# A fourth attention head's queries and keys in seven-product units, heads 40 steps apart, and small changes at the start and at the first convolution units

## The chip, the cores and the metric

The kernel runs on one core of a Trainium2 chip (eight cores, one used). The metric is the device time of one execution in microseconds, the median of several. Matmuls run on TensorE (PE, with weight loads shown as PEld), elementwise work on VectorE (DVE), ScalarE (ACT) and GpSimd (POOL); SyncE (SP) issues most DMAs.

## The reference

One streaming step of a one-layer hybrid encoder, in fp32, for 512 prompt frames and 64 sample frames (576 columns in all, D = 2048):

```python
hn = rmsnorm(x, g_norm1)
q, k, v, gb, gc, hc = jnp.split(hn @ w_in, ...)        # 6 x 1024 columns
q, k = rmsnorm(q, g_q), rmsnorm(k, g_k)                # per head, 8 heads x 128
o_attn = stick_breaking_blocks(q, k_all, v_all, P)     # weights: sigmoid(z) * prod(1 - sigmoid(z_j))
u = gc * hc
o_conv = gb * (conv_w[0]*u[t-2] + conv_w[1]*u[t-1] + conv_w[2]*u[t])
x = x + concat(rmsnorm(o_attn), rmsnorm(o_conv)) @ w_out
h2 = rmsnorm(x, g_norm2)
x = x + (silu(h2 @ w_gate) * (h2 @ w_up)) @ w_down     # D_FF = 5632
```

The sample frames also see 512 cached keys and values per head. Besides y the new keys, values and convolution states are outputs.

## The kernel before

Everything is kept transposed: channels on the 128 partitions, the 576 frames along the free axis in two halves of 288. A product of full precision is made from fp32r parts: an operand is split into a rounded high part (a ScalarE copy) and the remainder (a VectorE subtraction), and three matmuls (high x high, low x high, high x low) are summed.

**Plain projections.** `project` takes one 128-column weight through 2 halves x 16 k-tiles x 3 matmuls = 96 matmuls of 288 columns (`step`, L246). **Units.** Two columns at once can be made by a seven-product scheme (Strassen's, in Winograd's form): 7 products x 8 k-pairs x 3 = 168 matmuls (`unit_run`, L1047; `conv_run`, L1403; the feed-forward part, L1916). It needs sums of weight blocks (`unit_prepare`, `conv_prepare`) and sums of input blocks (`x_sums`, written to `xs_dram` by `store_sums` and read again by `load_sum` for the convolution part).

**Order.** PE's instructions are in the order of the program text. A `Pipeline` counts steps: `pipe.tick()` is called after each three matmuls, and generators that were spawned with a delay put out their next instructions at their step. So each engine's order follows from steps, and ACT, DVE, POOL and SP work through their own queues in order.

1. *Start* (L425 to L509). x arrives by column chunks (`XCH`), is turned by PE transposes (`turn_x`, L390), copied by ACT (L399, L401), scaled and split by DVE (L408, L409). The first projection's k-steps follow with a lag of three tiles, except that steps 0 and 1 run at tiles 1 and 3. Sums of squares of x (`square`, L419 on DVE for the last two chunks, L422 on ACT for the others) follow one by one, most of them after the loop.
2. `EARLY`: q and k of heads 0 and 1 as plain projections, stored to `qk_dram`.
3. `UNIT_COLS`: four units: v of heads 0 to 5 and q, k of head 2. Their weight blocks lie in five places that `call_blocks` refills.
4. `LATE`: twelve plain columns: q, k of heads 3 to 7 and v of heads 6, 7. Meanwhile `attend(h)` runs for all eight heads, head h spawned at step 1 + 49 h (`PERIOD`), each over 116 steps. Inside it `until(t)` waits to step t of that head. Its stations, by step before the change: load q and k (E, 0), cached keys (6), squares on ACT (8, 10), sums over 32 channels on DVE (12), their sum on PE (`ss`, L795, 22), the norm on DVE (23 to 29), scaling and splitting of q and k (30 to 35), key stores on SP (36), scores (48 to 55, L844 and L868), three logarithm steps on ACT for each key block, splits (55 to 64), sums over later keys (72, 75, 78: L919 to L937), each followed by `limit` (a mask on DVE, L893, an exponential on ACT, L895, and a cast), the last splits (76 to 81), the output product `po` (90, L951 and L954), the sample rows' sum `cz` (100) and product `os_` (112).
5. Two convolution groups as plain projections; after the first half of the third column `open_b` frees the heads' tiles and loads `xs_t1` and `xs_t2`.
6. Convolution units in the order of `corder`; after the first product `load_sum(3)` loads the last sums. `call_columns` loads weight columns (L1338) when a place is free.
7. Output projection, then gate and up units, then down units.

The change touches 1 (`square`, the loop), 3 (`UNIT_COLS`, `first_units`), 4 (`LATE`, `PERIOD`, `attend`, `late_evac`) and 6 (`load_sum` and its call).

Of the kernel before, what the change touches and what calls it, by code (L numbers as in the profile page):

```python
# [10 lines left out]
F32 = mybir.dt.float32  # L11
# [87 lines left out]
def tile_hybrid_stream_step(  # L99
# [314 lines left out]
    def square(c, i):  # L414
# [3 lines left out]
        if i < 4 and c >= len(XCH) - 2:  # L418
# [7 lines left out]
    with tc.manual_schedule(engines={mybir.EngineType.Activation, mybir.EngineType.DVE, mybir.EngineType.SP}):  # L426
# [3 lines left out]
        w0h, w0l = ready[0]  # L430

# [21 lines left out]
        for kt in range(KD + LAG):  # L453
# [22 lines left out]
            for c, (k0, k1) in enumerate(XCH):  # L476
# [274 lines left out]
    late_E = {}  # L751

    def attend(h):
# [9 lines left out]
        f, hi, lo, E = {}, {}, {}, {}  # L763
        for n, c in (("q", 0), ("k", 1)):
            if (c, h) in late_E:
                E[n] = late_E[c, h]
            else:
                E[n] = t1.tile([P, T], F32, tag="E" + n, name="E" + n)
                nc.sync.dma_start(out=E[n], in_=qk_dram[2 * h + c])
# [8 lines left out]
        yield until(8)  # L778
        for i, n in enumerate("qk"):
            if i:  # L780
                yield until(10)
            if (i, h) in EARLY:
                nc.vector.transpose(out=E[n], in_=E[n])
            f[n] = t1.tile([P, T], F32, tag=n + "f", name=n + "f")
            nc.scalar.activation(out=f[n], in_=E[n], func=AF.Square)
        yield until(12)
        for i, n in enumerate("qk"):
            nc.vector.reduce_sum(out=sums[:, NB * i : NB * (i + 1)], in_=chunks(f[n]), axis=mybir.AxisListType.X)
# [1481 lines left out]
```

## Time and profile before

| | |
|---|---|
| time, median of 3 runs | 2334.69 us (2334.25 to 2334.76) |
| the profiled execution | 2334.58 us, span 2332.9 us |
| PE busy | 2319.2 us (99%), 17445 matmuls |
| DVE busy | 1909.2 us (82%) |
| ACT busy | 1163.7 us (50%) |
| POOL busy | 278.5 us (12%) |
| HBM read, written | 303.23 MB, 95.86 MB |

A busy row is the union of an engine's instructions over the span. Matmuls overlap: each shows some 294 ns, though they start 132 ns apart. In the timeline a row has its start, its length, engine, line, operation, tiles written and read, sizes and count; in brackets stands the idle time of the engine ahead of it and what ended it. The groups have busy time and mean nanoseconds after the bar. The windows give, for each stretch, its length, then busy time (and instructions) of PE, PEld, DVE, ACT and POOL, the granted clock, the DMA engines' share and GB/s. By position the stages are: start 0 to 32 us, early projections to 72, units to 161, late projections with the heads to about 413, convolution to about 755, output projection to about 857, then feed-forward.

### The profile page before, as it was taken

To read this page: it belongs to the slowest core of one execution; us is meant where nothing else is said; L and a number is where in the kernel's file an instruction comes from. 1 tells how busy PE (TensorE), PEld (TensorE's weight loads), DVE (VectorE), ACT (ScalarE), POOL (GpSimd) and SP (SyncE) were. 2 spreads that over 40 slices of the span, in tenths; PEclk is the share of its full clock that TensorE was granted. 3 is DMA by queue.
4 is the path that set the end of the run, shared out by engine and by line. 5 is a ranking of instruction groups with operands and counts; after the bars stand their busy time and mean duration, and the time that the engine had idled before them with its cause. 6 is when DMAs were issued, how large, how long until landed. Compare 5 with 4: busy or idle time off the path is not lost.

```text
span 2332.9 us, 43682 instructions
## 1 busy us (share of the span) xinstructions
PE 2319.2 (99%) x17445; PEld 2309.7 (99%) x17445; DVE 1909.2 (82%) x2844; ACT 1163.7 (50%) x2007; POOL 278.5 (12%) x392
## 2 busy tenths in 40 slices
PE   9999999999999999999999999999999999999999
PEld 8999999999999999999999999999999999999999
DVE  8977776888887899888888888888888777887886
ACT  7537776444445565444444444444444444444444
POOL 2002332121111220000000000000000001431121
PEclk9999999999999999999999999999999999999999
DMA  8775554963478554444444444354344936885553
GB/s 276 208 226 144 142 142 127 309 199 106 129 245 247 166 174 144 155 129 149 142 138 153 125 151 156 110 158 150 123 154 135 363 114 214 220 239 192 198 135 101
DMA packets 584580, 401.93 MB, mean 172 GB/s; under 512 B 91775, under 2 KB 571769, under 8 KB 584377
## 3 DMA queue, kind: packets, MB, share of 16 engines
q1 hardware_dynamic: 573944, 378.27, 52.0%
q0 software_dynamic: 10064, 20.65, 3.9%
q8 instruction: 136, 2.23, 0.4%
q14 instruction: 68, 0.55, 0.1%
q10 hardware_dynamic: 368, 0.24, 0.0%
HBM read 303.23 MB, written 95.86 MB: 171 GB/s over the span
## 4 chain that ended last, share of the span: by engine, by line
PE 92%; DVE 4%; DMA 2%; ACT 2%; issue 1%; SPq 0%; POOL 0%; ACTq 0%; DVEq 0%; POOLq 0%
PE psy L1916 36%; PE psw L1916 18%; PE psx L1916 9%; PE pj L246 8%; PE psy L1403 6%; PE pjo L246 4%; PE psw L1403 3%; PE psy L1047 2%; PE psx L1403 1%; PE psw L1047 1%; PE psx L1047 1%; DMA Eq<-qk_dram 1%; DVE wlo L208 1%; DMA raw_a<-in_w_in_dram 0%; PE z L844 0%
## 5 line engine op out<-in xcount | busy, mean ns | idle before, releaser
L1916 PE MATMUL psy<-h_s,whl 128*128 128x288 f32 x2787 | 411.0, 294 | 0.0
L1916 PEld LDWEIGHTS psy<-h_s,whl 128*128 128x128 f32 x2787 | 383.4, 188 | 0.0
L256 DVE TENSOR_TENSOR whl<-raw_a,whl 128x1024 fp32r<-128x1024 f32 (+4 forms) x296 | 316.5, 1070 | 57.9 <-ACT whl L255 56.7
L1916 PE MATMUL psw<-t,whl 128*128 128x288 f32 x2400 | 347.6, 295 | 0.0
L1916 PEld LDWEIGHTS psw<-t,whl 128*128 128x128 f32 x2400 | 327.9, 188 | 0.2 <-DVE whl L256 0.2
L255 ACT CAST whl<-raw_a 128x1024 fp32r<-128x1024 f32 (+4 forms) x296 | 268.0, 906 | 101.6 <-issue 35.1
L246 PE MATMUL pj<-x,whi 128*128 128x288 f32 x1376 | 296.9, 299 | 0.4 <-DVE x L409 0.2
L256 DVE TENSOR_TENSOR whl<-raw_b,whl 128x1024 fp32r<-128x1024 f32 (+5 forms) x190 | 199.6, 1051 | 66.1 <-ACT whl L255 65.3
L255 ACT CAST whl<-raw_b 128x1024 fp32r<-128x1024 f32 (+5 forms) x190 | 165.4, 872 | 165.5 <-issue 73.1
L1926 ACT COPY part<-psy 128x288 f32<-128x288 f32 x242 | 96.6, 399 | 283.0 <-PE psy L1916 279.7
L246 PEld LDWEIGHTS pj<-x,whi 128*128 128x128 f32 x1376 | 227.7, 189 | 2.0 <-DVE x L409 1.1
L246 PE MATMUL pj<-x,wlo 128*128 128x288 f32 x688 | 203.7, 296 | 0.7 <-DVE wlo L182 0.6
L1916 PE MATMUL psy<-t2t,whl 128*128 128x288 f32 x1212 | 183.0, 294 | 0.0
L1916 PE MATMUL psy<-b22m,whl 128*128 128x288 f32 x1212 | 182.5, 294 | 0.0
L1916 PE MATMUL psx<-h_s,whl 128*128 128x288 f32 x1185 | 173.3, 294 | 0.0
L1916 PEld LDWEIGHTS psy<-t2t,whl 128*128 128x128 f32 x1212 | 168.2, 188 | 0.2 <-DVE whl L256 0.2
L1916 PEld LDWEIGHTS psy<-b22m,whl 128*128 128x128 f32 x1212 | 168.0, 188 | 0.0
L1916 PEld LDWEIGHTS psx<-h_s,whl 128*128 128x128 f32 x1185 | 162.6, 188 | 0.0
L246 PEld LDWEIGHTS pj<-x,wlo 128*128 128x128 f32 x688 | 129.7, 189 | 1.9 <-DVE wlo L182 0.9
L255 ACT CAST whl<-s 128x1024 fp32r<-128x1024 f32 (+5 forms) x81 | 72.3, 893 | 102.3 <-PE psw L1916 102.3
L1695 POOL DMA_DIRECT2D hid_dram<-form x3 | 2.3, 759 | 971.1 <-DVE form L256 971.1
L1916 PE MATMUL psy<-t,whl 128*128 128x288 f32 x576 | 106.8, 295 | 0.0
(534 smaller groups left out, 4482.5 us busy)
## 6 DMA issues: line engine op xcount, KB each, us to landing
hid_dram<-form SPq DMA_DIRECT2D x147, 288.0 KB, 2.5
raw_a<-in_w_in_dram SPq DMA_DIRECT2D x33, 1024.0 KB, 5.6
raw_a<-in_w_gate_dram SPq DMA_DIRECT2D x22, 1024.0 KB, 5.5
raw_a<-in_w_up_dram SPq DMA_DIRECT2D x22, 1024.0 KB, 5.6
raw_b<-in_w_gate_dram SPq DMA_DIRECT2D x22, 1024.0 KB, 6.4
raw_b<-in_w_up_dram SPq DMA_DIRECT2D x22, 1024.0 KB, 7.7
h_s<-hid_dram SPq DMA_DIRECT2D x10, 2016.0 KB, 11.3
raw_a<-in_w_out_dram SPq DMA_DIRECT2D x16, 1024.0 KB, 5.5
```

The costliest lines, as they stand in the source:

```text
L208: nc.vector.tensor_tensor(out=lo[:, a : a + 1024], in0=raw[:, a : a + 1024], in1=hi[:, a : a + 1024].bitcast(F32), op=ALU.subtract)
L246: mm(ps, w_[:, k, csl], x_, start=(k == 0 and n == 0), stop=(k == nk - 1 and n == 2))
L255: nc.scalar.copy(out=hi, in_=src)
L256: (lo_eng or nc.vector).tensor_tensor(out=lo, in0=src, in1=hi.bitcast(F32), op=ALU.subtract)
L1047: mm(ps, whl[:, w_, j, :], x_, start=(start and j == 0 and q == 0), stop=(j == NP - 1 and q == 2), skip_group_check=True)
L1403: mm(ps, whl[:, w_, j, :], x_, start=(start and j == 0 and q == 0), stop=(j == m - 1 and q == 2), skip_group_check=True)
L1695: q.dma_start(out=hid_dram[fp][2 * n - 2 : 2 * n].rearrange("f p t -> p f t"), in_=t.bitcast(F32))
L1916: mm(ps, whl[:, w_, j, :], x_, start=(start and j == 0 and q == 0), stop=(j == len(xs_) - 1 and q == 2), skip_group_check=True)
L1926: nc.scalar.copy(out=t, in_=st["y"])
```

## The change

- `UNIT_COLS` has a fifth unit, q and k of head 3; `LATE` loses these two columns and has another order. The places of the first weight blocks are called in another order.
- `PERIOD` is 40 and the stations in `attend` move; a head takes 109 steps. q and k are loaded apart, the squares go to a scratch area, and the key of head 7 is stored and loaded as the others are. The scaled fp32 copies of q and k, which had 576 columns, are kept for the last 192 columns alone: ACT writes the rounded copy straight from the unscaled one with the scale, and DVE makes the low part with the scale in a `scalar_tensor_tensor`.
- At the start eight products of a matrix of ones with itself are put in (5, 1 and 2), steps 0 and 1 of the first projection move to tiles 3 and 4, and the squares of the last chunk but one go from DVE to ACT.
- `load_sum(3)` is issued in two halves, after the first and the third product.

```diff
-UNIT_COLS = [[(2, 0), (2, 1)], [(2, 2), (2, 3)], [(2, 4), (2, 5)], [(0, 2), (1, 2)]]
+UNIT_COLS = [[(2, 0), (2, 1)], [(2, 2), (2, 3)], [(2, 4), (2, 5)], [(0, 2), (1, 2)], [(0, 3), (1, 3)]]
-LATE = [(0, 3), (1, 3), (0, 4), (1, 4), (0, 5), (1, 5), (2, 6), (0, 6), (1, 6), (0, 7), (1, 7), (2, 7)]
-PERIOD = 49
+LATE = [(0, 4), (1, 4), (0, 5), (1, 5), (0, 6), (1, 6), (0, 7), (1, 7), (2, 6), (2, 7)]
+PERIOD = 40
...
-        if i < 4 and c >= len(XCH) - 2:
+        if i < 4 and c == len(XCH) - 1:
...
+        warm = ps_pj.tile([P, HALF], F32, tag="pj", name="warm")
+        def keep_warm(n):
+            for _ in range(n):
+                mm(warm[:, :P], onef, onef, start=True, stop=True)
...
+                    keep_warm(1)
                     heads_of["s"] = turn_samples(0)
...
+                keep_warm(5)
                 turn_x(0, 0, 0, 0, None, first)
...
+            if kt == 2:
+                keep_warm(2)
...
-            k = {1: 0, 3: 1, 4: None}.get(kt, kt - LAG)
-            if k is not None and k >= 0 and (k or kt == 1):
+            if kt >= LAG:
                 for i, ps in enumerate(q0ps):
-                    step(ps, w0h, w0l, slice(0, P), x_two, k, KD, i)
+                    step(ps, w0h, w0l, slice(0, P), x_two, kt - LAG, KD, i)
...
+        def square_sums(i, n, t):
+            if (i, h) in EARLY:
+                nc.vector.transpose(out=E[n], in_=E[n])
+            sq = scratch[:, :T]
+            nc.scalar.activation(out=sq, in_=E[n], func=AF.Square)
+            yield until(t)
+            nc.vector.reduce_sum(out=sums[:, NB * i : NB * (i + 1)], in_=chunks(sq), axis=mybir.AxisListType.X)
+        fetch(0, "q")
         yield until(6)
+        fetch(1, "k")
+        yield until(9)
+        yield from square_sums(0, "q", 11)
+        yield until(14)
+        yield from square_sums(1, "k", 16)
+        yield until(18)
         cK = t1.tile([P, TP], F32, tag="cK", name="cK")
...
-        yield until(22)
+        yield until(24)
         ss = misc("ss")[:, : 2 * NB]
...
-        yield until(25)
+        yield until(27)
...
-            yield until(27 + 2 * i)
+            yield until(29 + 2 * i)
...
-        yield until(30)
-        nc.scalar.activation(out=qf, in_=qf, func=AF.Copy, scale=gqs)
-        cast(qh, qf[:, :TP])
-        yield until(32)
-        nc.scalar.activation(out=kf, in_=kf, func=AF.Copy, scale=col("gk"))
-        cast(kh, kf[:, : 3 * P])
-        yield until(33)
-        low(ql, qf[:, :TP], qh)
-        yield until(35)
-        low(kl, kf[:, : 3 * P], kh)
-        yield until(36)
-        nc.vector.transpose(out=cK, in_=cK)
+        for t, n, w in ((32, "q", gqs), (34, "k", col("gk"))):
+            yield until(t)
+            nc.scalar.activation(out=hi[n], in_=f[n][:, : cut[n]], func=AF.Copy, scale=w)
+            nc.scalar.activation(out=end[n], in_=f[n][:, 3 * P :], func=AF.Copy, scale=w)
+            yield until(t + 2)
+            stt(out=lo[n], in0=f[n][:, : cut[n]], scalar=w, in1=hi[n].bitcast(F32), op0=ALU.mult, op1=ALU.subtract)
+        yield until(37)
         put_tokens(E["k"], kp[:, h, :], 0, TP)
         put_tokens(E["k"], ks[:, h, :], TP, T)
+        yield until(39)
+        nc.vector.transpose(out=cK, in_=cK)
...
-        yield until(84)
+        yield until(82)
         sh = t1.tile([P, T], F32R, tag="sph", name="sph")
...
-        yield until(90)
+        yield until(87)
         po = misc("po")
...
-        yield until(100)
+        yield until(95)
         cz = misc("cz")
...
-        yield until(112)
+        yield until(105)
         os_ = misc("os")
...
-        call_blocks((2, 0, 1, 3, 4))
+        call_blocks((0, 2, 3, 4, 1))
...
-    def load_sum(q):
-        t = bt[q] = bt["pool"].tile([P, NP, 2, HALF], F32R, tag=f"t{q}", name=f"xs_t{q}")
-        nc.sync.dma_start(out=t.bitcast(F32), in_=xs_dram[q].rearrange("j f p t -> p j f t"))
+    def load_sum(q, j0=None):
+        if not j0:
+            bt[q] = bt["pool"].tile([P, NP, 2, HALF], F32R, tag=f"t{q}", name=f"xs_t{q}")
+        j0, j1 = (0, NP) if j0 is None else (j0, j0 + 4)
+        nc.sync.dma_start(out=bt[q][:, j0:j1].bitcast(F32), in_=xs_dram[q, j0:j1].rearrange("j f p t -> p j f t"))
...
-        if k_ == 0:
-            load_sum(3)
+        if k_ in (0, 2):
+            load_sum(3, k_ * 2)
```

The steps from 48 to 81 (scores, splits, sums over later keys, masks) stay where they were.

More of the change, by code (lines that the diff above doesn't have):

```diff
@@ L762, in attend, with fetch @@
         sums, ms, y, t_ = (scratch[:, 1856 + 36 * q : 1892 + 36 * q] for q in range(4))
[L763 to L769, printed above, removed]
+        f, hi, lo, E, end = {}, {}, {}, {}, {}
+        cut = {"q": TP, "k": 3 * P}
         def chunks(t, w=32):
             return t.rearrange("p (b c) -> p b c", c=w)
-        yield until(6)
+        def fetch(i, n):
+            E[n] = t1.tile([P, T], F32, tag="E" + n, name="E" + n)
+            nc.sync.dma_start(out=E[n], in_=qk_dram[2 * h + i])
+        def square_sums(i, n, t):
[6 more added lines that the diff above has]
+        fetch(0, "q")
+        yield until(6)
+        fetch(1, "k")
[4 more added lines that the diff above has]
+        yield until(18)
         cK = t1.tile([P, TP], F32, tag="cK", name="cK")
@@ L777, in attend @@
                               in_=ck[:, h, 32 * q : 32 * (q + 1)].rearrange("(b t) c -> t b c", t=32))
[L778 to L783, printed above, removed]
-            f[n] = t1.tile([P, T], F32, tag=n + "f", name=n + "f")
[L785 to L788, printed above, removed]
-        for n, e in (("q", TP), ("k", 3 * P)):
-            hi[n] = t1.tile([P, e], F32R, tag=n + "h", name=n + "h")
-            lo[n] = t1.tile([P, e], F32R, tag=n + "l", name=n + "l")
-        qf, qh, ql, kf, kh, kl = (x[n] for n in "qk" for x in (f, hi, lo))
-        yield until(22)
+        for n in "qk":
+            f[n] = t1.tile([P, T], F32, tag=n + "f", name=n + "f")
+            hi[n] = t1.tile([P, cut[n]], F32R, tag=n + "h", name=n + "h")
+            lo[n] = t1.tile([P, cut[n]], F32R, tag=n + "l", name=n + "l")
+            end[n] = t1.tile([P, T - 3 * P], F32, tag=n + "e", name=n + "e")
+        qf, qh, ql, qe, kf, kh, kl, ke = (x[n] for n in "qk" for x in (f, hi, lo, end))
+        yield until(24)
         ss = misc("ss")[:, : 2 * NB]
@@ L840, in scores @@
             if i == 3:
[L841 removed]
+                mm(zb[i], ke[:, :P], qe[:, :P], stop=False, **kw)
                 return
@@ L946, in attend @@
         cast(sh, sp)
-        yield until(86)
+        yield until(84)
         low(sl, sp, sh)
-        yield until(90)
+        yield until(87)
         po = misc("po")
@@ L1121, in evac @@
         def evac(ps, a, b):
-            if (c, h) == (1, NH - 1):
-                if not a:
-                    late_E[c, h] = t1.tile([P, T], F32, tag="Ek", name="Ek")
-                nc.vector.transpose(out=late_E[c, h][:, a:b], in_=ps)
-                return
             count[0] += 1
```

12 lines of the change are left out of this document (5 added, 7 removed).

## The prediction

> **What bounds the kernel now.** I read the page first (engines, chain), then PE's waits, then the timeline round each wait.
>
> ```profile
> span 2332.9 us, 43682 instructions
> PE 2319.2 (99%) x17445; PEld 2309.7 (99%) x17445; DVE 1909.2 (82%) x2844; ACT 1163.7 (50%) x2007; POOL 278.5 (12%) x392
> ```
>
> PE is busy 99% of the span and all else is behind it; a saved matmul shortens the run and a saved VectorE (DVE) or ScalarE (ACT) instruction does not, unless PE waits for it. What a matmul costs is read from the chain of waits, in order of time (start, length, what):
>
> ```profile
> 84.90 3.17 PE psy L1047 x24
> 423.38 39.55 PE pj L246 x299
> 476.12 11.65 DMA raw_a<-in_w_in_dram
> ```
>
> 24 matmuls take 3.17 us in a seven-product unit, 299 take 39.55 us in a plain projection: 132 ns each in both (the 294 ns that the groups show is latency). A step of the planner, three matmuls, is 0.40 us. PE's waits over the whole run (total, times, longest):
>
> ```profile
> PE psy L1403 <- DVE whl L1375: 2.1, 2, 1.3
> PE po L954 <- ACT ph L738: 0.7, 2, 0.4
> PE ss L795 <- DVE raw_a L788: 0.5, 1, 0.5
> ```
>
> So besides the matmul count only three places can give time: the start, the first convolution units and the heads. The profiled execution took 2334.58 us (span 2332.9 and 1.7 around it), the median of the three runs is 2334.69; I carry the sum over to the median.
>
> **Part 1, the fourth head's q and k in a unit.** Two plain columns are 2 x 2 x 16 x 3 = 192 matmuls, a unit is 7 x 8 x 3 = 168. 24 x 0.132 = **-3.17 us**. The unit adds some eight 128x1024 VectorE sums and splits against four splits; the units' stretch and one head period show whether they are hidden:
>
> ```profile
> 72.00:161.00 89.00, 89.00 (x675) 89.00 (x674) 72.77 (x92) 33.88 (x45) 2.18 (x4) 1.00 0.75 210
> 208.76:236.92 28.16, 28.16 (x210) 27.80 (x208) 21.60 (x40) 22.28 (x43) 7.12 (x17) 1.00 0.49 127
> ```
>
> Four units run there with PE never idle, DVE at 82%, ACT at 38%. A fifth is like them: nothing to add.
>
> **Part 2, the start.** PE's first x transposes, the first projection matmuls among them, and DVE's matching work:
>
> ```profile
> 3.81 1.09 PE L390 MATMUL psx<-ident,xin 128*128 128x128 f32 x4 [3.81 <-POOL acA L298]
> 8.60 0.61 PE L246 MATMUL pj<-x,wlo 128*128 128x288 f32 x1 [0.57 <-DVE wlo L182]
> 9.97 1.91 PE L390 MATMUL psx<-ident,xin 128*128 128x128 f32 x8
> 12.99 1.09 PE L390 MATMUL psx<-ident,xin 128*128 128x128 f32 x8
> 11.80 0.52 DVE L408 TENSOR_SCALAR x<-st,g1c 128x576 fp32r<-128x576 f32 x1 [1.86 <-ACT st L401]
> L373 SPq DMA_DIRECT2D xin<-in_x_prompt_dram x1: 507/507/507, 2.4 to 2.4; - x1
> DMA to landing us min/median/max: 5.7/5.7/5.7
> ```
>
> The transposes of tiles 2 and 3 run at 9.97 although their x, issued at 2.4, landed 5.7 us later, at 8.1: they stand behind step 0, which waits for a weight's low part. DVE then idles 1.86 us, and is dense from there to the end of the x tiles. After the change step 0 stands behind tile 3, so the transposes start at about 8.2 and DVE goes on at once. The eight transposes also take 1.91 us here and 1.09 us later: PE runs slow this early. The eight filler products lie in gaps: five before 3.81, the others before x of samples and tile 2 has landed.
>
> ```profile
> L868 PE MATMUL zs<-qf,cK 128*128 128x128 f32 x64 | 8.5, 275 | 0.0
> ```
>
> An fp32 128x128 product shows as two instructions of 133 ns, so eight are 2.1 us, perhaps 4 us at the slow rate; cover is 3.8 + 0.5 us. Without it they would cost the excess. The Trainium skill (TensorE: Matmul & The Clock Gate, Part 1: The HAM clock gate) has the array at half clock until about 3.4 us of sustained work. By that rule the fillers open the gate before tile 2; the slow transposes agree, though the granted clock of every window reads 1.00.
>
> Against it: four 128x512 squares go from DVE to ACT.
>
> ```profile
> 33.29 0.69 DVE L419 SCALAR_TENSOR_TENSOR xin<-xin 128x512 f32<-128x512 f32 x1
> 36.20 0.61 ACT L422 ACTIVATE xsn<-xsn 64x512 f32<-64x512 f32 x1
> 41.52 1.22 DVE L208 TENSOR_TENSOR wlo<-raw_a,whi 128x1024 fp32r<-128x1024 f32 x1
> 45.21 0.29 PE L246 MATMUL pj<-x,whi 128*128 128x288 f32 x1
> ```
>
> A square's time goes by its free size (512), so that is 4 x 0.61 = 2.4 us more in ACT's queue, ahead of the third weight's casts; DVE, 2.4 us lighter, waits for ACT's sums at the same place. The third weight's first low half is done at 42.74 for matmuls from 45.21: a slack of 2.5 us, which the 2.4 us use up. So of up to 1.9 us I take **-1.5 us** (ends -2.1 and 0).
>
> **Part 3, the last convolution sums in two halves.**
>
> ```profile
> 473.00:482.00 9.00, 9.00 (x70) 9.00 (x69) 8.06 (x8) 4.45 (x6) 0.00 (x0) 1.00 1.08 390
> 487.80 1.23 DVE L1361 TENSOR_TENSOR raw_a<-raw_a,raw_c 128x1024 f32<-128x1024 f32 x1 [1.62 <-DMA raw_a<-in_w_in_dram]
> 492.74 3.33 PE L1403 MATMUL psy<-xs_t,whl 128*128 128x288 f32 x23 [0.86 <-DVE whl L1375]
> 499.37 2.35 DVE L1375 TENSOR_TENSOR whl<-raw_a,whl 128x1024 fp32r<-128x1024 f32 x2
> 500.65 5.56 PE L1403 MATMUL psy<-x,whl 128*128 128x288 f32 x40 [1.27 <-DVE whl L1375]
> ```
>
> The weight column of the chain's DMA row (issued 476.12, landed 487.77) stands behind the sums' 8 x 2 x 128 x 288 x 4 = 2.36 MB. With half of that behind it, it lands 1.18 MB / 390 GB/s = 3.0 us sooner, DVE's 1.62 us wait goes, and with it PE's first stall. The second stall stays nearly whole: from 491 DVE works without a gap to the split at 499.37, which moves up by about as much as PE does. The second half has until product 4, at 494 or later. Gain 0.86 to 1.6: **-1.4 us** (ends -2.5, both stalls, and 0).
>
> **Part 4, heads 40 steps apart.** Nine steps fewer per head take 3.6 us off the 28.2 us of the period shown above; it holds 21.6 us of DVE, 22.3 of ACT. After: 24.6 us, DVE some 20.7 (9/32 of a column's two splits and two transposes less, 0.9), ACT at most 21.7. Nothing saturates; the order inside a head decides. Head 0's output product waited like this:
>
> ```profile
> 198.27 0.34 PE L937 MATMUL z<-s0l,neg1r 128*128 128x384 f32 x1
> 203.22 0.27 DVE L893 SCALAR_TENSOR_TENSOR z<-z,acA 128x128 f32<-128x128 f32 x1
> 203.24 0.38 PE L951 MATMUL po<-pr,vtok 128*128 128x128 f32 x2
> 204.16 0.34 PE L954 MATMUL po<-pl,vh 128*128 128x384 f32 x1
> 204.80 0.76 DVE L741 TENSOR_TENSOR pl<-pr,ph 128x512 fp32r<-128x512 f32 x1 [0.48 <-ACT ph L738]
> 204.82 0.50 PE L954 MATMUL po<-ph,vh 128*128 128x512 f32 x1 [0.32 <-ACT ph L738]
> ```
>
> The scores are complete at 198.61, but DVE masks them only at 203.22, 4.6 us later, behind the next head's norm (steps 23 to 29 of that head). From mask to last split are 2.3 us. With 40 steps that norm falls at steps 64 to 71, before the masks; in their place stand two low parts (0.7 and 0.6 us), so the mask runs 0 to 1.6 us late. The output product comes three steps (1.2 us) earlier. From the end of the scores to its last operand there are then 9 x 0.40 us and the products ahead of that operand (203.24 to 204.16 and three more, 1.5 us); less the 2.3 that leaves 2.8 us for the mask's lateness, so these stalls go. Head 0's first sum has its VectorE chain two steps longer and two steps later; its wait shrinks:
>
> ```profile
> 165.62 0.78 DVE L783 STREAM_TRANSPOSE Eq<-Eq 128x576 f32<-128x576 f32 x1 [4.03 <-DMA Eq<-qk_dram]
> 169.88 0.74 DVE L788 TENSOR_REDUCE raw_a<-kf 128x18 f32<-128x576 f32 x1
> ```
>
> It now blocks the weight's low half (1.2 us), which in the new order goes ahead of it. Together some 2 us go (the waits view's 1.2, and 0.2 to 0.3 more for each, since it counts idle from the modelled end of the last matmul: 204.16 to 204.82 lost 0.48, not 0.32).
>
> What comes: a head's squares and sums (steps 9 to 16) now fall among the previous head's scores, whose logarithms fill ACT. PE wants the key's sum eight steps (3.2 us) after it is put out, where it was ten.
>
> ```profile
> L205 ACT CAST whi<-raw_a 128x1024 fp32r<-128x1024 f32 x23 | 22.9, 1043 | 0.0
> ```
>
> A weight's two casts (2.1 us) stand at step 7 of each column of 32, a head starts at 1 + 40h: in heads 2 and 6 they fall on its step 54 (81 + 54 = 128 + 7), just before the next head's key square, and I take 1 us lost in each, at the sum or at the sample rows' product. Also all loads of a next head stand behind eight key stores on SP:
>
> ```profile
> 205.04 4.83 SPq L726 DMA_DIRECT2D out_dram<-Ek  x8
> 210.03 0.35 SPq L769 DMA_DIRECT2D Eq<-qk_dram  x1
> ```
>
> Issued at step 37 they last to step 47, so q's load starts some 3 us late and lands about when its square is due at step 9. Scaling into the rounded copies and 192 columns takes ACT from 2048 to 1280 columns a head; PE does not feel it. I set stalls gone against stalls new: **0 us** (ends -2, nothing new, and +6, a new 1 us in every head).
>
> **Sum:** -3.17 - 1.5 - 1.4 + 0 = -6.1: 2334.69 - 6.1 = **2328.6 us**.
>
> **Rivals.** *The heads take some back (0.2):* every head waits 0.6 us at its sum or at the product for the sample rows, 8 x 0.6 - 2 = +2.8: 2331.4. For it: the work packed into the score window; against it: PE never idles in the period shown, with much the same work. *Only the matmuls go (0.17):* ACT's squares eat the start, and the weight's load is held by its own wait on DVE, not by the queue: 2334.69 - 3.2 = 2331.5. *The masks stay late (0.07), slower:* if DVE's backlog before the last mask keeps head 0's 4.6 us in all heads, past the 2.8 us that are left, each head loses 1.8 us, 14.4 - 2 = +12.4 against -6.1: 2341.0. For it speaks POOL:
>
> ```profile
> 175.89 1.73 DVE L741 TENSOR_TENSOR ql<-qf,qh 128x512 fp32r<-128x512 f32 x1
> 175.83 1.24 POOL L810 TENSOR_TENSOR Ek<-Ek,rpad_t 128x576 f32<-128x576 f32 x1 [3.88 <-ACT qh L738]
> ```
>
> Beside POOL's key scaling this split of 512 columns took 1.73 us; one of the same size took 0.76 alone (204.80). After the change the scaling falls right before the masks. The Trainium skill (Advanced Engine Details and Errata, VectorE Performance Modes, Mode Summary) says that the second Vector SBUF port is shared with GpSimd and the two block each other; by it this delay returns in every head, about 1 us, which is under the 2.8. The pair of rows agrees.
>
> **Chances.** Forecast 0.56, its own range 2326 to 2330.5. 0.2% is 4.7 us, about what a measurement of this kernel can tell from no change; faster means under 2330.0. The forecast case lies there nearly always (0.52), the second and third in a third of their cases (0.06): faster 0.58; slower 0.07; same 0.35. Range: the low end adds the better ends of parts 2 to 4 in part (-9), the high end takes in both middle rivals and part of +6: 2325.7 to 2334.0.
>
> **What would show it.** Right: 24 fewer unit and projection matmuls beside eight filler products; DVE with no gap near 10 us; no wait of DVE on the weight's DMA near 480 and one PE stall, not two, in the first convolution units; no wait on the ph cast in the heads. Wrong: PE waits at sums in most heads, masks over 2.8 us behind their scores, or ACT's casts late for the third projection.

## The result and the profile after

The changed kernel takes 2357.18 us (median of 5 runs, 2354.72 to 2358.92); the kernel before, beside it, 2334.69. The ratio is 1.0094, 95% interval 1.0083 to 1.0105: slower by 22.5 us where 6 us less were forecast. The profiled execution took 2357.18 us. Its page, span and engines:

```profile
span 2355.1 us, 43712 instructions
PE 2329.8 (99%) x17437; PEld 2314.5 (98%) x17437; DVE 1916.4 (81%) x2846; ACT 1163.5 (49%) x2021; POOL 273.8 (12%) x394
```

The matmuls are 8 fewer: 24 fewer for the unit, 16 more instructions for the fillers, as announced. Everything else has to be looked for by stage. Windows cut at the first unit matmul, the last one, the first matmul of the convolution units and their last (columns: window, length, busy time and count of PE, PEld, DVE, ACT and POOL, granted clock, DMA share, GB/s). First the kernel before:

```profile
0.00:72.05 72.05, 66.26 (x479) 63.56 (x479) 63.44 (x140) 55.13 (x149) 13.27 (x30) 1.00 0.83 275
72.05:160.77 88.72, 88.72 (x674) 88.72 (x672) 72.72 (x92) 33.83 (x45) 2.18 (x4) 1.00 0.74 210
160.77:462.88 302.11, 300.73 (x2215) 295.80 (x2214) 226.71 (x415) 200.53 (x389) 81.62 (x154) 1.00 0.61 172
462.88:754.96 292.08, 289.95 (x2190) 289.37 (x2189) 233.81 (x326) 135.15 (x217) 49.98 (x60) 1.00 0.62 187
```

and then the changed one:

```profile
0.00:73.57 73.57, 70.00 (x495) 67.26 (x495) 59.83 (x130) 57.17 (x155) 13.34 (x30) 1.00 0.83 269
73.57:184.50 110.93, 110.93 (x842) 110.93 (x840) 89.50 (x112) 42.61 (x56) 4.34 (x8) 1.00 0.68 193
184.50:484.30 299.80, 284.69 (x2023) 274.63 (x2022) 217.89 (x404) 189.50 (x384) 76.78 (x151) 0.98 0.59 165
484.30:777.00 292.70, 290.62 (x2190) 289.48 (x2189) 234.73 (x329) 135.42 (x218) 46.96 (x62) 1.00 0.62 188
```

- The start is 1.5 us longer (73.57 against 72.05).
- The units are 22.2 us longer, which is one unit, 88.72 / 4, with PE never idle: hidden, as forecast.
- The head stage has lost 192 matmuls, 192 x 0.132 = 25.4 us, so it should take 302.1 - 25.4 = 276.7 us. It takes 299.8: **23.1 us are lost there**, the whole loss of the run. PE is idle for 15.1 us of the stage, and the mean granted clock is 0.98.
- The convolution units are 0.6 us longer (292.70 against 292.08); the gain forecast for them does not show in this one execution.

Where PE stands, in the waits of the changed kernel (total, times, longest):

```profile
PE po L964 <- DVE pl L750: 10.4, 14, 2.1
PE ss L808 <- DVE raw_a L786: 3.2, 2, 2.9
PE os L984 <- issue: 1.4, 2, 0.7
...
PE ps_r1s L532 <- DVE rpad_t L523: 1.0, 1, 1.0
```

The output product waits 14 times for the last splits; before it waited twice, 0.7 us. What holds the splits is seen round the masks of one head, head 3. A head has three masks; the last one's scores are complete at 307.01, and this is what "late" is counted from below. DVE in the changed kernel:

```profile
306.23 0.60 DVE L903 SCALAR_TENSOR_TENSOR z<-z,acA 128x128 f32<-128x128 f32 x2
308.50 0.75 DVE L830 SCALAR_TENSOR_TENSOR ql<-qf,gqs,qh 128x512 fp32r<-128x512 f32 x1 [1.68 <-ACT qh L827]
309.17 0.29 DVE L903 SCALAR_TENSOR_TENSOR z<-z,acA 128x128 f32<-128x128 f32 x1
309.37 0.61 DVE L830 SCALAR_TENSOR_TENSOR kl<-kf,vec,kh 128x384 fp32r<-128x384 f32 x1
...
310.24 0.29 DVE L903 SCALAR_TENSOR_TENSOR z<-z,acA 128x128 f32<-128x128 f32 x1
...
312.79 1.23 DVE L208 TENSOR_TENSOR wlo<-raw_a,whi 128x1024 fp32r<-128x1024 f32 x1 [1.21 <-ACT whi L205]
313.94 0.68 DVE L750 TENSOR_TENSOR pl<-pr,ph 128x512 fp32r<-128x512 f32 x1
```

and ACT beside it:

```profile
306.92 0.49 ACT L905 ACTIVATE pr<-z 128x384 f32<-128x384 f32 x1 [3.57 <-DVE z L903]
307.44 0.41 ACT L747 CAST ph<-pr 128x256 fp32r<-128x256 f32 x1
307.75 0.72 ACT L827 ACTIVATE qh<-qf,gqs 128x512 fp32r<-128x512 f32 x1
...
311.72 1.99 ACT L205 CAST whi<-raw_a 128x1024 fp32r<-128x1024 f32 x2
```

Read the two together. DVE's first mask at 306.23, behind the next head's norm, frees ACT, which had been idle for 3.57 us. ACT makes its exponential and cast and only then scales the next head's q (307.75), because the scaling was put behind them in its queue (step 32 of the next head is step 72 of this one). DVE has the low part of that q next in its own queue, so it idles 1.68 us, and the second mask, whose input has long been there, stands behind it. The third mask stands behind the key's low part in the same way (310.24, 3.2 us behind the scores), and the last split behind a weight's low half that waits for ACT's casts. The output product's last operand comes at 314.6, and PE has waited 2.08 us for it. In this head that weight is the last link: the cast that the split reads was done at 311.8 (311.19 and 0.62), so without the weight's low half between them the split would have ended at some 312.5, when PE got there. Over all eight heads DVE's waits for the scaling are, in the changed kernel and then before:

```profile
DVE ql L830 <- ACT qh L827: 9.2, 7, 1.7
...
DVE ql L741 <- ACT qh L738: 3.8, 7, 0.6
DVE kl L741 <- ACT kh L738: 3.2, 6, 0.5
```

In sum they are not much more than before (9.2 against 7.0 us), but the single wait is up to three times as long, and it now stands among the masks. From the end of a head's scores to its last mask the heads 0 to 6 take 4.1, 4.7, 4.3, 3.2, 4.7, 5.9 and 4.4 us (before 4.6, 2.2, 4.6, 2.2, 4.1, 1.7, 3.3).

To the waits comes the granted clock, which halves three times in the stage. Windows of one 3.4 us period before each fall, and the period after it:

```profile
214.20:217.60 3.40, 0.81 (x6) 0.84 (x7) 1.76 (x4) 2.65 (x6) 0.80 (x2) 1.00 0.93 207
217.60:221.00 3.40, 3.40 (x17) 3.40 (x16) 3.01 (x10) 2.37 (x7) 1.40 (x3) 0.51 0.27 78
...
364.40:367.80 3.40, 1.43 (x9) 0.96 (x7) 2.61 (x7) 3.37 (x8) 0.70 (x1) 1.00 0.46 76
367.80:371.20 3.40, 3.02 (x10) 2.56 (x10) 2.67 (x6) 1.23 (x3) 0.15 (x1) 0.50 0.71 131
```

A period in which PE was busy for 0.81 or 1.43 of 3.4 us is followed by one at half clock. Three such periods cost about 3 x 1.7 = 5.1 us. So of the 23.1 us some 15 are waits in the view and 5 the clock. I put the remaining 3 down to what the waits view leaves out of each wait; that is an estimate.

### The profile page after: what moved, and what is told of

It is laid out like the page before. It is cut to its first block, busy times and chain, and to the rows that moved or that the text cites. A ratio compares the mean times of both kernels' runs of the same rounds, so it can differ in the third digit from the quotient of the medians.

```text
span 2355.1 us, 43712 instructions
## 1 busy us (share of the span) xinstructions
PE 2329.8 (99%) x17437; PEld 2314.5 (98%) x17437; DVE 1916.4 (81%) x2846; ACT 1163.5 (49%) x2021; POOL 273.8 (12%) x394
## 4 chain that ended last, share of the span: by engine, by line
PE 87%; DVE 5%; ACT 3%; DMA 2%; issue 1%; SPq 1%; POOL 0%; DVEq 0%; ACTq 0%; POOLq 0%
PE psy L1923 35%; PE psw L1923 18%; PE psx L1923 9%; PE psy L1410 6%; PE pjo L246 4%; PE pj L246 4%; PE psw L1410 3%; PE psy L1057 3%; PE psx L1410 2%; PE psw L1057 1%; PE psx L1057 1%; DMA form_dram<-hf 1%; DMA raw_a<-in_w_out_dram 1%; SPq L465 0%; DVE pl L750 0%
## 5 line engine op out<-in xcount | busy, mean ns | idle before, releaser
L256 DVE TENSOR_TENSOR whl<-raw_a,whl 128x1024 fp32r<-128x1024 f32 (+4 forms) x296 | 321.4, 1087 | 56.0 <-ACT whl L255 55.1
L246 PE MATMUL pj<-x,whi 128*128 128x288 f32 x1248 | 272.2, 301 | 0.3 <-DVE x L409 0.3
L246 PEld LDWEIGHTS pj<-x,whi 128*128 128x128 f32 x1248 | 209.0, 191 | 1.3 <-DVE x L409 0.6
L246 PE MATMUL pj<-x,wlo 128*128 128x288 f32 x624 | 185.8, 298 | 0.1
L246 PEld LDWEIGHTS pj<-x,wlo 128*128 128x128 f32 x624 | 118.7, 190 | 1.1 <-DVE wlo L494 0.3
```

Of the source, the lines that this page charges most:

```text
L246: mm(ps, w_[:, k, csl], x_, start=(k == 0 and n == 0), stop=(k == nk - 1 and n == 2))
L256: (lo_eng or nc.vector).tensor_tensor(out=lo, in0=src, in1=hi.bitcast(F32), op=ALU.subtract)
```

## The experiments

My theory after the comparison: **order**. At 40 steps the next head's scaling falls among the masks, and two engines that each work in order hand each other's delay on. Rivals: the new stations cost by themselves at any distance; or DVE and ACT have too much work for 40 steps. All runs were timed against the kernel before on the same chip. "Head stage" is from the last matmul of the head-mode units to the first of the convolution units in each profile (276.7 us is what 40 steps would take without loss). It is read from the one profiled execution, which lies up to some 3 us from the median (2352.24 in a_scale_late, 2343.26 in d_all, 2335.36 in e_split, 2337.56 in f_last), so steps of a few us are to be taken from both columns together.

```
run           median us  ratio to before [95%]     head stage us
after         2357.18    1.0094 [1.0083, 1.0105]   299.8
a_start       2335.49    1.0002 [0.9993, 1.0011]   (before's heads)
b_warm        2334.78    1.0000 [0.9991, 1.0009]   (before's heads)
b_square      2335.83    1.0003 [0.9994, 1.0012]   (before's heads)
a_load        2333.11    0.9992 [0.9983, 1.0000]   (before's heads)
a_heads50     2336.70    1.0008 [0.9999, 1.0017]   302.1 (50 steps)
a_scale_late  2349.68    1.0067 [1.0054, 1.0079]   296.4
b_keys        2387.98    1.0224 [1.0210, 1.0238]   333.4
b_all         2387.18    1.0224 [1.0210, 1.0238]   331.3
c_fill        2355.67    one run                   300.3
c_pre         2348.75    1.0063 [1.0051, 1.0076]   293.3
c_pre22       2341.10    1.0032 [1.0021, 1.0044]   284.4
c_pre41       2364.03    1.0122 [1.0107, 1.0138]   306.7
d_start       2339.03    1.0018 [1.0009, 1.0027]   284.4
d_po          2348.74    1.0064 [1.0052, 1.0077]   294.1
d_all         2340.14    1.0029 [1.0016, 1.0041]   286.2
e_split       2337.72    1.0013 [1.0004, 1.0022]   281.1
e_best        2348.29    1.0060 [1.0047, 1.0072]   294.5
f_last        2335.67    1.0002 [0.9993, 1.0011]   281.3
```

### The start alone: a_start, b_warm, b_square

a_start is the kernel before with the diff's edits in the start; b_warm has the fillers alone, b_square one line:

```diff
-        if i < 4 and c >= len(XCH) - 2:
+        if i < 4 and c == len(XCH) - 1:
```

> The kernel before with the new start alone (eight filler products, step 0 behind tile 3, one chunk of squares moved from DVE to ACT). Theory: the profile of the changed kernel has the loop over the x tiles end at the same time and the row scale 1.1 us late on PE, so +1.5 us: 2336.2. Rival, the step as predicted: -1.5, 2333.2.

> The kernel before with the eight filler products alone. Theory: they do not open the clock sooner for good, and the three that stand in no gap cost at most 1 us: 2335 to 2336. Rival, the rule of an earlier clock: the x transposes at full rate, 2333.5 or less.

> The kernel before with one chunk's four squares moved from DVE to ACT alone. Theory: ACT's squares end 2.5 us later, PE waits 1.1 us at the row scale: 2336. Rival, they lie beside other work: 2335.0, as before.

By the times alone none can be told from no change. The traces can tell: the first unit matmul comes at 71.8 to 73.3 us (mean 72.4) in the nine profiles with the old start, and at 73.1 to 74.5 (mean 73.8) in the nine with the whole new one; 74.3 with the squares alone, 72.9 with the fillers alone. The squares are the cost. DVE's first sum over all squares, before

```profile
38.60 0.19 DVE L501 TENSOR_REDUCE ssr<-ssx 128x5 f32<-128x35 f32 x1
```

and in b_square:

```profile
41.86 0.19 DVE L501 TENSOR_REDUCE ssr<-ssx 128x5 f32<-128x35 f32 x1 [4.83 <-ACT xsn L422]
```

Before, DVE ended its squares at 38.3 and ACT at 38.6, side by side. Now ACT ends at 41.8 and DVE has nothing to do for 4.83 us. The row scale is late with it, and PE waits 0.9 us for it in b_square (1.0 in the changed kernel). In all ten profiles with the moved squares DVE idles 4.83 or 4.84 us at this place, and the sum comes at 40.7 to 42.1; in the ten others it doesn't idle, and the sum comes at 38.3 to 39.8.

### The last sums in two halves: a_load

The kernel before with `load_sum(3, 0)` after the first and `load_sum(3, 4)` after the third product.

> The kernel before with the last sums loaded in two halves alone. As predicted: -1.4, 2333.3, PE's first stall near 491 (1.1 us start to start) gone and the second smaller. Rival: the weight column's landing is not set by the 2.36 MB ahead of it, no change within 0.2 us.

1.9 us less, interval 0 to 4.0. DVE's wait for the weight column's DMA (1.62 us before) is gone, and with it the first stall near 491; the second, 1.4 us from start to start, is 0.4. A stall of 1.2 us stands at 472 instead, ahead of the load in question: DVE's work there was some 1.5 us later in this execution. From the first to the 312th unit matmul the five profiles with the whole load take 43.2 to 44.5 us (mean 43.9), of the fifteen with halves fourteen take 41.8 to 43.6 (mean 42.5), and one 46.2, with a period at half clock and new waits. Over the whole stage the means are 292.4 and, without that one, 290.9 us; single profiles scatter by 2 and 3 us in the two groups.

### The new stations at a distance: a_heads50

The changed `attend` with four units, the twelve columns in their old order, the old start and load:

```diff
-PERIOD = 40
+PERIOD = 50
```

> The changed heads (all new stations, 192 fp32 columns) with the old columns (four units, twelve late columns), the old start and the load in one piece; heads 50 steps apart, so that step 32 of a head stands at step 82 of the one before, behind its masks. Theory (it is the distance: the next head's scaling falls among the masks): masks at most 2 us behind their scores, no wait at the output product over 0.5 us, 2334.7 to 2337. Rival (the new stations cost by themselves, at any distance): waits of 1 to 2 us per head stay, over 2345.

The stage takes 302.1 us, as before to a tenth; the last masks are 0 to 2.8 us late; the output product waits 1.8 us in all, at most 0.7 at a time (both somewhat over what was expected). At this distance the stations, the scaling into rounded copies and the 192 fp32 columns cost nothing. What is left is the distance, with all that 40 steps bring beside each other, the columns' weight splits too.

### The scaling behind the masks: a_scale_late

```diff
-        for t, n, w in ((32, "q", gqs), (34, "k", col("gk"))):
+        for t, n in ((39, "q"), (41, "k")):
...
-            yield until(t + 2)
+        for t, n in ((42, "q"), (44, "k")):
```

> The changed kernel with one thing moved: the scaling of q and k from steps 32 and 34 to 39 and 41, their low parts from 34 and 36 to 42 and 44, the cached keys' transpose from 39 to 45, all behind the three masks of the head before. Theory (DVE stands in order behind low parts that wait for ACT's scaling, which waits for the previous head's exponentials): masks at most 2 us late, the 13 us of waits at the output product go and with them the three times that the granted clock halves (5 us): 2357.2 - 18 = 2339, between 2336 and 2345. Rival (the masks are late for DVE's backlog of the norm before them, or for the weight's casts on ACT): less than 5 us gained, over 2352.

7.5 us come back by the times, between the two expectations; in the two profiles the head stage is 3.4 us shorter. The waits in this kernel:

```profile
PE ss L808 <- DVE raw_a L786: 7.5, 5, 2.6
PE z L856 <- DVE kl L835: 2.3, 5, 1.3
PE os L986 <- issue: 2.2, 2, 1.3
...
PE po L966 <- DVE pl L750: 1.1, 2, 0.9
```

At the output product the mechanism is confirmed: 10.4 us became 1.7 (with 0.6 of another row), the last masks are 1.5 to 3.7 us late instead of 3.2 to 5.9, and DVE's wait for the scaled q is gone. But with PE no longer held there, the next head's sum `ss` became the place to wait: 7.5 us after 3.2. Together with the key's low part this takes back most of it, so that PE's idle time in the stage falls only from 15.1 to 13.7 us, and the clock halves twice instead of three times. SP's queue shows why the sums wait:

```profile
336.32 5.66 SPq L735 DMA_DIRECT2D out_dram<-Ek  x8
342.16 0.35 SPq L778 DMA_DIRECT2D Eq<-qk_dram  x1
342.61 0.40 SPq L189 DMA_DIRECT2D raw_a<-in_w_in_dram  x1
343.30 1.83 SPq L778 DMA_DIRECT2D Ek<-qk_dram  x1
```

The next head's loads stand behind eight key stores, which themselves wait for POOL's scaling of the keys, which waits for the norm. ACT then idles 3.35 us for q (to 345.12), and does k's square at 349.94, behind two score blocks' logarithm steps.

### The stores on another queue: b_keys, b_all

Both are built on a_scale_late. Besides the edit shown, b_keys has the key's square at steps 11 and 13 instead of 14 and 16; b_all also moves the values' low part and the sample rows' product.

```diff
-        yield until(37)
-        put_tokens(E["k"], kp[:, h, :], 0, TP)
-        put_tokens(E["k"], ks[:, h, :], TP, T)
+        yield until(33)
+        put_tokens(E["k"], kp[:, h, :], 0, TP, nc.gpsimd)
+        put_tokens(E["k"], ks[:, h, :], TP, T, nc.gpsimd)
```

> The kernel with the scaling behind the masks (2349.7), and two things more: the eight stores of the normed keys go out on POOL's queue at step 33 instead of SP's at 37, so that nothing stands ahead of the next head's loads, and the key's square goes from steps 14 and 16 to 11 and 13, ahead of two logarithms on ACT. Theory (the loads behind the stores, and ACT's order, make the five waits at the sums, 7.5 us, and one clock closing): most of that goes, 2341 to 2344. Rival (POOL's DMA issues hold its affine selections and the columns' stores, or the loads land late for another reason): over 2348.

> The same, and besides: the values' low part from step 67 to 80, behind the masks, and the sample rows' product from 105 to 107. Theory: masks earlier by about 1 us, the waits at the key's low part (2.3 us) and at the sample rows' product (2.2 us) go too: 2337 to 2340, still above before for the start's loss and for a clock closing or two. Rival (the low part now holds the output product): as the run without it or slower.

Both are 38 us slower than a_scale_late; the rival had it. POOL's queue in b_keys:

```profile
299.47 0.69 POOL L735 DMA_DIRECT2D out_dram<-Ek  x1 [0.45 <-POOL Ek L823]
303.61 0.68 POOL L735 DMA_DIRECT2D out_dram<-Ek  x1 [3.44 <-issue]
306.09 0.66 POOL L735 DMA_DIRECT2D out_dram<-Ek  x1 [1.80 <-issue]
308.53 2.77 POOL L735 DMA_DIRECT2D out_dram<-Ek  x5 [1.79 <-issue]
```

Eight stores that SP puts out in 4 to 5.7 us take POOL 11.8 here, with a pause of 1.8 to 3.4 us after each of the first three. The key's buffer is free only after them, so the next k lands at 315.5, ACT idles 6.36 us for it, and the sums wait 27.5 us in all. Half clock takes another 44 us of windows, some 22 us lost. What else b_all moved can't be read beside this.

### The query ahead of the stores: c_pre, and the norm sooner: c_pre22

c_pre lets each head put out the next head's q load at its step 33, ahead of its key stores (SP's again), squares q at 5 and k at 11, and makes the sample rows' product at 107. c_pre22 besides:

```diff
-        yield until(24)
+        yield until(22)
         ss = misc("ss")[:, : 2 * NB]
...
-        yield until(27)
+        yield until(25)
```

> The kernel with the scaling behind the masks (2349.7; the keys' stores on SP again), and the next head's query load put out at step 33, ahead of the eight key stores, its square at 5 and 6, the key's square at 11 and 13, the sample rows' product at 107. Theory (SP's queue and ACT's order make the waits at the sums): of the 7.5 us at the sums over half goes, of the 2.2 at the sample rows too, 2342 to 2345. Rival (the key's load, still behind the stores, is what the sums wait for): within 2 us of 2349.7.

> As the run before it, and the sum and norm two steps sooner (22, 25, 27, 29), so that key scaling, stores and the key's load come sooner too. If the sums wait for a load that is late by more than two steps this is 2 to 6 us slower than the run before it; if the norm's place ahead of the masks is what is left, 1 to 3 us faster.

In c_pre the waits at the sums are gone, but the output product's are back (6.2 us for splits, 1.8 more in other rows): 0.9 us gained, a wait moved, not removed. The sum no longer held PE back, so the norm ran into the masks, and the last masks are up to 6.2 us late again. With the norm two steps sooner they are late by 0.7 to 2.9 us in heads 1 to 6, the clock never falls in the stage, and 7.7 us come back (8.9 in the stage). Head 0's is still 5.2 us late. So the norm just ahead of the masks was the second half of the cause; the key's stores and load come two steps sooner with it, but in c_pre the sums no longer waited for them. My expectation for c_pre was wrong: I had taken the wait at the sum for a cost of its own; it was also what kept the norm's place tolerable.

### One step more: c_pre41

> As c_pre with heads 41 steps apart, the most that ends with the last column: 0.4 us more for each head's work at no more matmuls. If each head lacks a fraction of a microsecond (a queue full to the brim): 2 to 4 us faster than c_pre. If single columns' casts fall badly, the time moves either way by 1 to 3 us, with the waits in other heads.

15 us slower than c_pre. More time for each head is not better by itself. PE waits 9.9 us for the key's low part alone, its idle time in the stage is 17.5 us instead of 10.7, and the clock stands at half for 20.5 us instead of 3.4, which costs some 8.5 us more. So by these numbers over half of the 15 us is the clock, and the waits ahead of it are what has to be explained. That the casts of the columns' weights (step 7 of every 32) fall elsewhere against heads of 41 steps is the likely reason, and only argued.

### Filling a wait: c_fill

```diff
         ss = misc("ss")
+        for _ in range(10 if h == 1 else 0):
+            mm(ss[:, :P], onef, onef, start=True, stop=True)
```

> The changed kernel with ten 128x128 fp32 filler products (20 instructions, 2.7 us) ahead of the sum of head 1, into a bank that the sum then overwrites. There PE waits 3.0 us in the changed kernel, and 0.8 us after its end the granted clock falls to half for 3.4 us. Theory (the idle time closes the clock): no half clock near 217 to 221 us, the other two stay, span 1 to 2 us shorter. Rival (the clock falls for another reason, or by chance): half clock there all the same, and the fillers cost nothing or up to 1 us.

The fall at 217 us does not occur; the 3.0 us wait shrank to 0.35. But the clock fell at 315.1, where it had not before, at 366.3, and at 397.0 for two periods: four at half clock where the changed kernel's profile has three. So the saved fall doesn't show in the time (2355.67 lies within the range of the changed kernel). One execution can't prove that the idle time closes the clock; it agrees with it, and the periods counted at the end are the stronger evidence.

### What is left: d_start, d_po, d_all, e_split, e_best, f_last

d_start is c_pre22 with the old start. d_po adds two steps to the output product (87 to 89). d_all and e_split, with and without d_po's edit, move the weights' splits of three late columns out of the masks:

```diff
+    SPLIT = {2: 20, 6: 14, 7: 20}
...
-        yield 7
+        d = SPLIT.get(i - len(EARLY), 7) if i >= len(EARLY) else 7
+        yield d
```

> The best so far (2341.1: scaling behind the masks, query load ahead of the stores, norm at 22 to 29) with the old start. Theory (the new start costs 1 to 2 us in any surroundings): 2339 to 2340. Rival (the start is free): 2341.

> The same with the output product two steps later (89, its copy at 90). Theory (its operands come 0.7 to 1.4 us late in three heads, and two steps are 0.8 us): 2 to 2.5 us less than d_start, 2337. Rival (the wait only moves on to the next head's scores, since DVE and ACT set the pace there): as d_start.

> The same, and in the three late columns whose weight is split at step 7 to 11 among a head's masks (third, seventh, eighth), the split put off to step 20, 14 and 20. Theory (a weight's casts, 2 us on ACT, and low halves, 2.4 us on DVE, among the masks make what is left of the waits): 2 to 4 us less than d_po, 2333 to 2335. Rival (moved, they hold the logarithms or the next weight's load): as d_po or slower.

> The 2339.0 kernel (old start, scaling behind the masks, query load ahead of the stores, norm sooner) with the splits of the third, seventh and eighth late column moved to steps 20, 14 and 20; the output product stays at 87. Theory (the splits among the masks make the 0.9 to 1.5 us waits in every fourth head): 4 us less, 2335, level with before. Rival (the waits move on to the scores, as with the later output product): 2338 or more.

The old start gives 2 to 3 us (2339.0 against 2341.1, ratios 1.0018 and 1.0032). d_po is 9.7 us slower, which neither expectation had: the wait moved to the next head's scores, which stand one step ahead of the product now, and three periods at half clock, some 5 us, came with it:

```profile
PE z L855 <- ACT kh L830: 7.6, 6, 2.5
PE z L855 <- DVE kl L834: 3.9, 6, 1.4
```

With the splits moved as well 8.6 us of that go (d_all), and without d_po's edit 1.3 us (e_split, where 4 were expected). e_best then puts ACT's two fp32 end copies behind the key's rounding, the first head's sum at 24 and the sample rows' product at 109; f_last is the same with that product at 107.

> The same, and: the two fp32 end copies on ACT behind the key's rounding, not between (0.4 us sooner for the key's low part in five heads), the first head's sum back at 24 (0.9 us), the sample rows' product at 109 (1.1 us). Theory: 2 to 4 us less than e_split, 2331 to 2333, faster than before by 1 to 3 us. Rival (each wait moves on): as e_split.

> e_split with the end copies on ACT behind the key's rounding and the first head's sum at 24; the sample rows' product at 107 as there. Theory (the loss was order alone): waits in the heads under 2 us in all, 3 to 6 us less than e_split, 2331 to 2334, faster than before by 1 to 4 us. Rival (the waits move on once more): 2336 to 2338, as e_split.

In e_best the sample rows come out wrong: at 109 the next head's logarithms (its step 68, this head's 108) overwrite the weights that the product reads. It also has to wait for them, 14.2 us; all other waits in the heads are under 0.3 us. f_last in the heads:

```profile
PE po L969 <- DVE pl L744: 1.4, 2, 1.2
...
PE os L989 <- issue: 0.8, 1, 0.8
PE z L859 <- DVE kl L838: 0.8, 4, 0.2
```

It takes 2335.67 us, level with before (1.0002, 0.9993 to 1.0011), 21.5 us under the changed kernel. The unit, the 40 steps and the load in halves are all kept; with another order in the heads and the old start the loss is gone. The expected 1 to 4 us below before did not come: the stage takes 281.3 us. The last 4.6 us to 276.7 use up the unit's 3.2 and the load's 1.4; most of them are waits (by the starts of matmuls 6.6 us in 23 places, against 2.8 in 10 before; the view above shows about half). I found no 40-step order in these runs that beats the kernel before; the one kernel below it is a_load, the load in halves alone, 2333.11 us, at the edge of what can be told.

## Why the prediction was wrong, point by point

- **Part 1, the unit, -3.17 us: right.** Five units of 22.2 us without a gap, two columns of 12.7 us fewer.
- **Part 2, the start, -1.5 us: wrong, +1.4 us** in the traces' means. The transposes were sooner (8.97 against 9.97 in the changed kernel) but tile 4 reached DVE hardly sooner (14.30 against 14.42), since step 0 now stood ahead of its transposes, and the first projection was done at 31.85 us against 31.80. The failing sentence is the one on the squares: I priced them at the third weight's low half (slack 2.5 us, used up) and not at the sum that needs all of them. DVE and ACT had ended together there, so 2.4 us more on ACT made it 2.5 us later (38.60 before, 41.10 in the changed kernel), whatever DVE does. The range's upper end, 0, was too low as well.
- **Part 3, the load, -1.4 us: right as far as can be told.** -1.5 by the means of the traces, -1.9 (-4.0 to 0) by the time. The first stall went by the step named. The second, which was to stay nearly whole, shrank from 1.4 to 0.4 as well, so the agreement of the sum is in part luck: the stall at 472 took the surplus in a_load.
- **Part 4, the heads, 0 us: wrong, +23.1 us.** The step that failed: "With 40 steps that norm falls at steps 64 to 71, before the masks; in their place stand two low parts (0.7 and 0.6 us), so the mask runs 0 to 1.6 us late". I charged the two low parts their own durations. But each waits for ACT, and ACT's scaling stood behind the exponential of the mask before it: three masks and two low parts on two engines, at whose end the last mask was 3.2 to 5.9 us late in heads 0 to 6. The step before it also failed: the norm did end before the masks by step, but DVE was still at it when they were due, and c_pre22 shows that to be worth 7.7 us. The margin of 2.8 us was about right: masks 1.5 to 3.7 us late left 1.7 us of waits in a_scale_late. The loads behind the key stores were named and taken as harmless (landing "about when its square is due"; the 4.83 us shown for the stores are twelve steps, not ten). As the order stood they were mostly hidden behind the greater wait; 7.5 us of waits stood there as soon as that was gone, though taking these away gained 0.9 us by itself. The clock's falls, 5 us, had no term at all. How the 23 us divide between scaling, norm and loads can't be said: each wait covered another. That it is the order in the heads is shown by f_last.
- **The rivals.** "The masks stay late, slower" had the sign, the place and the mechanism in outline (masks past the margin in every head), for 2341.0. Its price was 1.8 us a head where 23.1 / 8 = 2.9 were lost, because it knew neither the clock's falls (5 us) nor the sums. What spoke for it, the split of q slowed beside POOL, did not come in every head. It took 1.73 us in head 0 alone, where no masks stand yet, and 0.75 to 0.83 in the seven others; among head 3's masks (308.50) it was late, not slow. In heads 1 and 5, where the split began first, POOL's key scaling beside it took 1.78 and 1.51 us instead of 1.24. What the Trainium skill says on the shared port (Advanced Engine Details and Errata, VectorE Performance Modes, Mode Summary; there of Vector instructions in the two-port modes), weighed there, is thus not what decided here.
- **The chances.** 0.07 for slower came from pricing each collision alone. The period row had DVE at 21.6 and ACT at 22.3 us of 28.2; in 24.6 us they are busy for 0.84 and 0.88 of the time by the forecast's own numbers, which leaves little room to make up a wait that one passes to the other. That row was a reason for a larger chance, though f_last shows that the busy shares alone don't decide it. There is a slip in the sum too: a third of 0.2 and 0.17 is 0.12, not 0.06, so faster should have been 0.64 by its own terms.

What stays open: why PE waits so much more at 41 steps, how the loss divides between the steps of the order, and whether some order at 40 steps takes the last 4.6 us.

## What to carry to other kernels

When work is moved next to other work on in-order engines, price it by when its input comes, not by its own length: look up what the moved instruction waits for, what that stands behind, and what then stands behind it. A wait that is removed shows the next one; before believing the gain, find the second-latest operand at the same place, and expect the removed wait to have covered something else. Work moved off a busy engine must be followed to the sum that needs the last piece, and compared with when the other engine gets to it.

## What the runs showed of the hardware

**The clock falls on a fixed grid, for less than a whole idle period.** All changes of the granted clock in the heads lie whole multiples of 3.413 us apart (217.6, 367.8, 398.5 in the changed kernel: 44 and 9 periods). PE's idle time was counted, from the starts of matmuls, in each period of seven profiles (after, a_scale_late, b_keys, c_fill, c_pre, c_pre41, d_po). Of the periods at full clock, every one with 2.3 us or more idle was followed by one at half clock, and none with less than 1.7; in between it went either way. The border shifts by some 0.2 us with how the short pauses between matmuls are counted. Once at half, the clock stayed there for a second period in a few cases with less idle. The Trainium skill (TensorE: Matmul & The Clock Gate, Part 1: The HAM clock gate) gives the same free-running 3413 ns and a fall after at least one idle window; here some 60% of a window idle was enough. So a wait of a little over 2 us can cost 1.7 more, or nothing, by where it lies in the grid.

**The fillers opened the clock sooner, and lost it again.** In a_start, c_fill, c_pre and c_pre22 the clock opened at 4.5 to 5.1 us, fell 3.4 us later while PE waited for x, and opened for good at 11.3 to 14.8; in the other profiles with fillers, and in those without, it opened once, at 10.8 to 14.0. It gained nothing: the first unit matmul came at 73.1 to 74.5 us in these four, and at 73.4 to 74.5 in the five others with the whole new start.

**POOL put these stores out more slowly than SP.** Eight stores of a head's keys take 10.2 to 11.9 us on POOL in the sixteen heads of b_keys and b_all, and 3.9 to 5.7 us on SP in a_scale_late. In b_keys each head has pauses of 1.8 us or more after its first three stores and none after the others; why is open.
